# Where the modulation sums run: out of the attention's column projections, unevenly over the three branches, with a prioritised final addition

## The chip, the cores and the metric

The kernel runs on one core of a Trainium2 chip. A core has a matrix engine (TensorE, PE in the profile, with its weight loads as PEld), VectorE (DVE), ScalarE (ACT), GpSimd (POOL), and SyncE (SP), which here only issues transfers. Each engine has a queue of its own and works through it in order; they wait for one another by semaphores. The metric is the device time of one execution in microseconds (us); lower is better.

## What is computed

One layer of a conditioned decoder trunk in float32, 512 tokens of width 1024. From the conditioning vector `c` come six modulation vectors, and the layer uses them as shift, scale and gate of its two halves:

```python
mod = (c @ ada_w[l] + ada_b[l])[:, None, :]          # c: 1024, ada_w: 1024 x 6144
sh1, sc1, g1, sh2, sc2, g2 = jnp.split(mod, 6, axis=-1)
h = rmsnorm(x, norm_mix[l]) * (1 + sc1) + sh1
z = h @ w_in[l]
...
o_attn = dsa_attention(z_attn, positions, rel_bias)   # per query the 128 best-scored keys
o_rwkv = rwkv7_mix(z_rwkv, ...)
o_conv = c_b * causal_dwconv(c_c * c_x, sc_conv_w[l])
gates = jax.nn.sigmoid(z_gate).reshape(b, s, N_BRANCH, D_MODEL)
merged = sum(gates[:, :, i] * (o @ w_branch[l, i]) for i, o in enumerate((o_attn, o_rwkv, o_conv)))
x = x + g1 * (merged @ w_o[l])
h = rmsnorm(x, norm_ffn[l]) * (1 + sc2) + sh2
x = x + g2 * conv_glu_ffn(h, ffn_w_up[l], ffn_conv_w[l], ffn_w_down[l])
```

`sh1` and `sc1` are needed at the start. `g1`, `sh2`, `sc2` and `g2`, the last two thirds of `mod`, are needed only once the three branches are merged. The change is about when these late ones are computed.

## The kernel before

**Matrix products.** Each weight tile is loaded by SP (`wraw`, L147 in `load_raw`, four buffers), rounded by ACT to a high half `whi` (L163), and the rest, the low half `wlo`, is made by a subtraction (L169): on POOL up to the last branch, on DVE in it (`lo_engine`). Activations are split in the same way. Each product is then three matmuls (L181 to L183), 512 columns each. `whi` and `wlo` have three buffers. Results go to PSUM banks, three named `mm` and five named `sd`.

**Modulation sums** (`ada_parts`, L200 to L226). A generator with 64 steps: eight groups of 512 outputs (four columns of `modc`), each of eight steps. One step has SP load 256 KB of `ada_w` into `xraw` (three buffers) and DVE multiply it by one column of `c` and add it to `acc` (L219 for the first step of a group, L221 for the other seven; two buffers of `acc`). At step k = 4 of the following group, `finish` sums the group over the partitions by four one-column matmuls (L206, into an `mm` bank) and DVE adds the bias (L207), which frees the bank.

Who calls the generator sets where a step stands: `att_cols`, the projection of q, k and the index queries to DRAM (`z_att`), does one step for each of the four column blocks of slot 1 (the keys); `branch`, which makes the gates and the output product of one branch, does four steps for each of its eight gate blocks. What is left runs out in later calls, which then do nothing. The calls before come to 4 in `att_cols`, 32 in `branch(1)`, 28 in `branch(2)`, none in `branch(0)`.

**Order of the program.** Projections; scoring of the index keys; the selection (L842 to L844): for each of three query blocks, 16 rounds of `max` (eight largest of each row, `m8`) and `match_replace` (mark them) on the score tile `sc`; the attention (L855 to L898): four head pairs, each with loads of `qs`, `kh` and `kl` on POOL's queue, and per query block a load of the bias `bt` on SP's, an addition of the mask on POOL (L869), score matmuls (L817), the logits on DVE (L876), the exponential on ACT (L878), transposes on PE (L885), and the value product; then `branch(1)` (RWKV), `branch(2)` (convolution), `branch(0)` (attention), and the feed-forward half.

The written order is only a priority. A scheduler lays the instructions into the engines' queues, by program order as priority and by when operands are ready; `tc.high_priority(offset=...)` moves a piece ahead. So `branch(1)`, `branch(2)` and the steps called in them fill the queues beside the selection and the attention, which stand earlier in the program: in the order built, `branch(1)` runs during the selection and parts of `branch(2)` and its modulation steps lie before, in and behind the attention.

Of the kernel before, what the change touches and what calls it, by code (L numbers as in the profile page):

```python
# [16 lines left out]
ALU = mybir.AluOpType  # L17
# [42 lines left out]
def hybrid_block(ctx, tc, ins, out, consts, dbg=None, stop=99):  # L60
    nc = tc.nc
    PE, ACT, DVE, POOL, SP = nc.tensor, nc.scalar, nc.vector, nc.gpsimd, nc.sync
# [7 lines left out]
    def dram(name, offset, ap):  # L70
        t = ins[name]
        return bass.AP(tensor=t.tensor, offset=t.offset + offset, ap=ap)

    def mm_bank():
        return pp.tile([128, 512], F32, name="mm", tag="mm", bufs=3)

    def sd_bank():
        return pp.tile([128, 512], F32, name="sd", tag="sd", bufs=5)

    def T(name, shape, dt=F32, tag=None, bufs=1, pool=None):  # L80
        return (pool or sb).tile(shape, dt, name=name, tag=tag or name, bufs=bufs)
# [49 lines left out]
    def cv(name, i=0, n=1):  # L131
        tag, r = col[name]
        return colv[tag][:, r + i:r + i + n]
# [7 lines left out]
    def load_raw(shape, srcs, own=None):  # L141
        if own is None:
            raw = wp.pool.tile(shape, F32, name="wraw", tag="wraw", bufs=n_raw)
        else:
            raw = own[0].tile(shape, F32, name="xraw", tag="xraw", bufs=own[1])
        for dst, ap in srcs:
            SP.dma_start(dst(raw), ap)  # L147
        return raw
# [26 lines left out]
    def mm_t(ps, w, act, k0=0, start=True, stop=True):  # L175

        hi, lo = w
        ahi, alo = act
        kt = hi.shape[1]
        for k in range(kt):  # L180
            PE.matmul(ps, hi[:, k, :], ahi[:, k0 + k, :], start=start and k == 0, stop=False)  # L181
            PE.matmul(ps, hi[:, k, :], alo[:, k0 + k, :], start=False, stop=False)  # L182
            PE.matmul(ps, lo[:, k, :], ahi[:, k0 + k, :], start=False, stop=stop and k == kt - 1)  # L183
# [12 lines left out]
    def wk():  # L196
        return T("wk", [128, 512], tag="wk", bufs=4)


    def ada_parts():  # L200


        def finish(acc, o):
            pm = mm_bank()
            for i in range(4):
                PE.matmul(pm[:, i:i + 1], acc[:, i * 128:(i + 1) * 128], one, start=True, stop=True)  # L206
            DVE.tensor_tensor(modc[:, o:o + 4], pm[:, 0:4], cv("ada_b", o, 4), op=ALU.add)  # L207
            if o == 36:
                DVE.scalar_tensor_tensor(modc[:, 32:40], modc[:, 32:40], 1.0, cv("norm_ffn", 0, 8), op0=ALU.add, op1=ALU.mult)

        done = None
        for o in range(16, 48, 4):
            acc = T("acc", [128, 512], pool=adp.pool, bufs=2)
            for k in range(8):
                raw = load_raw([128, 512], [((lambda r: r), dram("ada_w", k * 128 * 6 * D + o * 128, [[6 * D, 128], [1, 512]]))],
                               own=(adp.pool, 3))
                ck = ccol[:, k:k + 1]
                if k == 0:
                    DVE.tensor_scalar(acc, raw, ck, None, op0=ALU.mult)  # L219
                else:  # L220
                    DVE.scalar_tensor_tensor(acc, raw, ck, acc, op0=ALU.mult, op1=ALU.add)  # L221
                if done and k == 4:
                    finish(*done)
                yield
            done = acc, o
        yield  # L226
        finish(*done)

    ada = ada_parts()

    def rsqrt_of(v, n):
# [25 lines left out]
    modc = T("modc", [128, 48])  # L257
# [50 lines left out]
    pm = sd_bank()  # L308
# [97 lines left out]
    def z_col(c0, n=128):  # L406
        w = w_in(c0, n)
        ps = mm_bank()
        mm_t(ps[:n], w, hT)
        return ps  # L410
# [50 lines left out]
    for p in range(4):  # L461
        i = p % 2
# [11 lines left out]
        k, r, kn, km, P, iP = (E(n, [128, 512]) for n in ("k", "r", "kn", "km", "P", "iP"))  # L474
# [51 lines left out]
        for c0 in (0, 4):  # L526
            for hh in range(2):
                q = halves[hh][0]
                ps = sd_bank()
                for c in range(c0, c0 + 4):  # L530
                    o = (c - c0) * 128
# [21 lines left out]
        for c0 in (0, 4):  # L553
            ps = sd_bank()
            for c in range(c0, c0 + 4):
                o = (c - c0) * 128
# [27 lines left out]
    for rnd in range(2):  # L584
        for u0 in (0, 16):
            ps = sd_bank()
            for u in range(u0, u0 + 16):
                for hh in range(2):
                    b = hh * 64
                    o = slice((u - u0) * 32, (u - u0) * 32 + 32)  # L590
# [15 lines left out]
    for c in range(8):  # L606
# [19 lines left out]
        for p in range(4):  # L626
            for hh in range(2):
                o = (p * 2 + hh) * 64
# [14 lines left out]
        if c:  # L643
            for p in range(4):
                for hh in range(2):
                    q, z = halves[hh]
                    o = (p * 2 + hh) * 64
# [107 lines left out]
    def split_out(dst, ps, scale):  # L755
        n = ps.shape[0]
        hi = T("wk", [128, 512], F32R, tag="wk", bufs=4)
        lo = T("wk", [128, 512], F32R, tag="wk", bufs=4)
        ACT.activation(hi[:n], ps, AF.Copy, scale=scale)
        DVE.scalar_tensor_tensor(lo[:n], ps, scale, hi[:n], op0=ALU.mult, op1=ALU.subtract)  # L760
        ACT.dma_start(dst[:, 0, :], hi[:n].bitcast(F32))
        SP.dma_start(dst[:, 1, :], lo[:n].bitcast(F32))

    def att_cols(c0, slot, scale):
        for i in range(4):
            if slot == 1:
                next(ada, None)
            if slot < 2:
                next(bias, None)
            split_out(z_att[slot, i], z_col(c0 + i * 128), scale)  # L770

    def load_q(dst, z, t0, n):

        row = 2 * 512
        for hh in range(2):
            src = bass.AP(tensor=z.tensor, offset=z.offset + hh * 512 + t0, ap=[[row, 64], [64 * row + (1 - 2 * hh) * 512, 2], [1, n]])
            POOL.dma_start(dst[hh * 64:(hh + 1) * 64], src)

    att_cols(C_ATT + 3 * MIX, 2, HD ** -0.5)
    ps = z_col(C_ATT + 4 * MIX, 72)  # L780
    split_out(z_ki, ps[0:64], 1.0)
# [129 lines left out]
    def branch(i, o, first, last):  # L911
        for m2 in range(4):
            gate = []
            for m in range(2):
                ps = z_col(C_GATE + i * D + (m2 * 2 + m) * 128)
                sg = wk()
                if first:
                    ACT.activation(sg, ps, AF.Sigmoid)
                else:
                    ACT.activation(sg, ps, AF.Tanh, scale=0.5)  # L920
                for _ in range(4):
                    next(ada, None)
                gate.append(sg)
            for m in range(2):
                mm = m2 * 2 + m
                w = weights("w_branch", i * MIX * D, D, 0, 4, [(mm * 128, 128)])
                ps = mm_bank()
                mm_t(ps, w, o)
                dst = merged[:, mm, :]
                if first:  # L930
                    ACT.activation(dst, ps, AF.Copy, scale=2.0)  # L931
                    POOL.tensor_tensor(dst, dst, gate[m], op=ALU.mult)
                    continue
                DVE.scalar_tensor_tensor(gate[m], gate[m], 1.0, ps, op0=ALU.add, op1=ALU.mult)
                DVE.tensor_tensor(dst, dst, gate[m], op=ALU.add)
                if last:
                    ACT.activation(mg_hl[0][:, mm, :], dst, AF.Copy, scale=0.5)
                    DVE.scalar_tensor_tensor(mg_hl[1][:, mm, :], dst, 0.5, mg_hl[0][:, mm, :], op0=ALU.mult, op1=ALU.subtract)

    def split_o(src):  # L940
# [4 lines left out]
        return o  # L945

    branch(1, split_o(o_rw), True, False)
    branch(2, split_o(o_cv), False, False)
    lo_engine[0] = DVE
# [376 lines left out]
```

## Time and profile before

| what | us |
| --- | --- |
| median of three runs | 1160.54 |
| the three runs | 1160.04, 1160.54, 1165.31 |
| the profiled execution, its own time | 1152.93 |
| span of that execution (first to last instruction) | 1150.9 |
| mean granted TensorE clock of that execution | 0.968 |

The profile shows one execution, hence its own time, below the median. The stretches of that execution that matter here: the last selection runs on DVE from about 465 to 515 us; the attention on PE from 534 to 626; the last branch, `branch(0)`, from 640 to 707. A busy share is an average over stages; a wait counts where PE, which is busy nearly throughout, has one.

### The profile page before, as it was taken

Reading aid. Unit: us, or ns where it says so; the run is one execution under the profiler, and the core shown is the slowest. Engines: PE = TensorE matmul, PEld = TensorE weight load, DVE = VectorE, ACT = ScalarE, POOL = GpSimd, SP = SyncE. Lnnn points to the kernel's source line nnn. Section 1 sums busy time; section 2 is a strip of 40 time slices with the busy share of each in tenths; the row PEclk is TensorE's granted clock in tenths of the full one; section 3 lists DMA queues with packets and bytes.
Section 4 is the critical chain, followed back from the end, with each engine's and each line's share of the span. In section 5 each row is a group of like instructions: output and inputs, shape, how many; then the busy total and the mean of one; then the engine's idle time right before and its main releaser. Section 6 shows DMA issues by size and latency. Waiting matters only on the chain.

```text
span 1150.9 us, 17786 instructions
## 1 busy us (share of the span) xinstructions
PE 1066.1 (93%) x6822; PEld 877.9 (76%) x6822; DVE 715.9 (62%) x1331; ACT 467.8 (41%) x786; POOL 342.0 (30%) x259
## 2 busy tenths in 40 slices
PE   4889999999899999977889999988999999999996
PEld 3667788777666877855678888878988898888885
DVE  5847766432699769993534435579767666652316
ACT  4255544332334344233444334356434443542213
POOL 4211111222363235654555000125344545100001
PEclk9789999999999999988899999998999999999999
DMA  9764467922548952689875334531333233462201
GB/s 328 199 147 97 106 130 161 217 73 75 133 125 248 284 166 67 183 225 243 210 157 168 104 91 139 154 110 38 92 111 97 65 95 101 157 219 92 92 1 73
DMA packets 194689, 160.32 MB, mean 139 GB/s; under 512 B 18563, under 2 KB 167453, under 8 KB 194605
## 3 DMA queue, kind: packets, MB, share of 16 engines
q1 hardware_dynamic: 162589, 122.55, 37.1%
q0 software_dynamic: 8960, 22.11, 9.9%
q10 hardware_dynamic: 23056, 14.53, 4.1%
q8 instruction: 53, 0.87, 0.3%
q14 instruction: 31, 0.25, 0.1%
HBM read 129.53 MB, written 18.63 MB: 129 GB/s over the span
## 4 chain that ended last, share of the span: by engine, by line
PE 62%; DVE 15%; DMA 9%; issue 8%; POOL 3%; ACT 3%; SPq 0%; POOLq 0%; DVEq 0%; ACTq 0%
PE mm L181 8%; PE mm L182 8%; PE mm L183 8%; DMA wraw<-in_ffn_w_up 2%; DMA xraw<-in_ada_w 2%; PE sd L181 2%; PE sd L182 2%; PE sd L183 2%; PE sd L1250 2%; PE sd L1252 2%; PE sd L1251 2%; PE sd L734 1%; DVE wlo L1017 1%; DMA bt<-bias_d 1%; PE sd L1047 1%
## 5 line engine op out<-in xcount | busy, mean ns | idle before, releaser
L182 PE MATMUL mm<-h_lo,whi 128*128 128x512 f32 (+2 forms) x496 | 198.3, 400 | 1.6 <-DVE h_lo L1076 1.5
L181 PE MATMUL mm<-h_hi,whi 128*128 128x512 f32 (+2 forms) x496 | 198.9, 402 | 0.3 <-ACT merged L931 0.3
L183 PE MATMUL mm<-h_hi,wlo 128*128 128x512 f32 (+2 forms) x496 | 198.6, 401 | 0.0
L163 ACT ACTIVATE whi<-wraw 128x1024 fp32r<-128x1024 f32 (+1 forms) x86 | 80.3, 935 | 204.3 <-PE mm L182 116.9
L169 POOL TENSOR_TENSOR wlo<-wraw,whi 128x1024 fp32r<-128x1024 f32 (+2 forms) x49 | 115.9, 2367 | 150.3 <-ACT whi L163 138.6
L182 PEld LDWEIGHTS mm<-h_lo,whi 128*128 128x128 f32 (+1 forms) x496 | 93.9, 189 | 21.1 <-DVE h_lo L1076 2.0
L183 PEld LDWEIGHTS mm<-h_hi,wlo 128*128 128x128 f32 (+1 forms) x496 | 94.0, 189 | 19.4 <-issue 0.2
L181 PEld LDWEIGHTS mm<-h_hi,whi 128*128 128x128 f32 (+1 forms) x496 | 93.7, 189 | 19.1 <-ACT merged L931 0.8
L1017 DVE TENSOR_TENSOR wlo<-wraw,whi 128x1024 fp32r<-128x1024 f32 x46 | 64.9, 1411 | 61.1 <-ACT whi L1016 60.4
L1016 ACT ACTIVATE whi<-wraw 128x1024 fp32r<-128x1024 f32 x46 | 48.6, 1057 | 78.6 <-DMA wraw<-in_ffn_w_up 28.1
L221 DVE SCALAR_TENSOR_TENSOR acc<-xraw,ccol,acc 128x512 f32<-128x512 f32 x56 | 62.9, 1122 | 26.0 <-DMA xraw<-in_ada_w 25.7
L1034 POOL TENSOR_TENSOR fS<-wraw 128x512 f32<-128x512 f32 x13 | 20.3, 1565 | 180.1 <-DVE wk L991 108.2
L1047 PE MATMUL sd<-mg_hi,shi 128*128 128x256 f32 x156 | 45.2, 289 | 8.9 <-DVE p L1190 8.9
L167 POOL DMA_DIRECT2D wlo<-wraw x21 | 18.2, 867 | 116.9 <-ACT wlo L166 111.7
L728 DVE TENSOR_SCALAR mk<-posq,thr 128x512 f16<-128x512 f32 (+3 forms) x128 | 47.1, 441 | 2.0 <-PE sd L734 2.0
L1017 DVE TENSOR_TENSOR slo<-wraw,shi 128x1024 fp32r<-128x1024 f32 x28 | 34.7, 1239 | 21.4 <-ACT shi L1016 21.4
L1293 POOL TENSOR_TENSOR f<-f 128x512 f32<-128x512 f32 x4 | 5.7, 1417 | 135.0 <-ACT wk L993 135.0
L181 PE MATMUL mm<-o,whi 128*128 128x512 f32 x96 | 39.9, 416 | 6.2 <-DVE modc L207 6.2
L181 PE MATMUL sd<-h_hi,whi 128*128 128x512 f32 x112 | 45.4, 405 | 0.0
L182 PE MATMUL sd<-h_lo,whi 128*128 128x512 f32 x112 | 45.3, 404 | 0.0
L183 PE MATMUL sd<-h_hi,wlo 128*128 128x512 f32 x112 | 45.0, 402 | 0.0
L1049 PE MATMUL sd<-mg_hi,slo 128*128 128x256 f32 x156 | 44.6, 286 | 0.0
(525 smaller groups left out, 2813.2 us busy)
## 6 DMA issues: line engine op xcount, KB each, us to landing
wraw<-in_w_in SPq DMA_DIRECT2D x61, 512.0 KB, 4.7
xraw<-in_ada_w SPq DMA_DIRECT2D x96, 256.0 KB, 4.2
wraw<-in_ffn_w_up SPq DMA_DIRECT2D x44, 512.0 KB, 4.2
wraw<-in_ffn_w_down SPq DMA_DIRECT2D x22, 512.0 KB, 3.5
wlo<-wraw POOLq DMA_DIRECT2D x21, 512.0 KB, 5.3
wraw<-in_w_branch SPq DMA_DIRECT2D x24, 256.0 KB, 3.1
bias_d<-stage ACTq DMA_DIRECT2D x10, 512.0 KB, 7.3
wraw<-in_w_o SPq DMA_DIRECT2D x8, 512.0 KB, 3.8
```

The lines of the kernel that those rows point to most:

```text
L163: ACT.activation(hi, raw, AF.Copy)
L169: lo_engine[0].tensor_tensor(lo, raw, hi, op=ALU.subtract)
L181: PE.matmul(ps, hi[:, k, :], ahi[:, k0 + k, :], start=start and k == 0, stop=False)
L182: PE.matmul(ps, hi[:, k, :], alo[:, k0 + k, :], start=False, stop=False)
L183: PE.matmul(ps, lo[:, k, :], ahi[:, k0 + k, :], start=False, stop=stop and k == kt - 1)
L221: DVE.scalar_tensor_tensor(acc, raw, ck, acc, op0=ALU.mult, op1=ALU.add)
L728: DVE.tensor_scalar(m_[:, :n], posq[:, b * 128:], thr[:, b, gg:gg + 1], None, op0=ALU.is_ge)
L1016: ACT.activation(hi, src, AF.Copy)
L1017: DVE.tensor_tensor(lo, src, hi, op=ALU.subtract)
L1047: PE.matmul(ps, w[0][:, k], b[0][:, k], start=first and k == 0, stop=False, skip_group_check=True)
L1049: PE.matmul(ps, w[1][:, k], b[0][:, k], start=False, stop=k == 3, skip_group_check=True)
L1250: PE.matmul(ps, hi, w[0][:, c], start=first, stop=False)
```

## The change

It does four things. `finish` is called at the end of the following group's eight steps in place of after the fifth. Its bias addition is issued with high priority. `att_cols` no longer calls the generator. And each gate block of a branch calls it three times in `branch(0)`, once in `branch(1)` and five times in `branch(2)`, in place of four times: 8 steps in `branch(1)`, 40 in `branch(2)`, the last 16 and the end in `branch(0)`.

```diff
-            DVE.tensor_tensor(modc[:, o:o + 4], pm[:, 0:4], cv("ada_b", o, 4), op=ALU.add)
+            with tc.high_priority(offset=4000):
+                DVE.tensor_tensor(modc[:, o:o + 4], pm[:, 0:4], cv("ada_b", o, 4), op=ALU.add)
...
-                if done and k == 4:
+                if done and k == 7:
                     finish(*done)
...
     def att_cols(c0, slot, scale):
         for i in range(4):
-            if slot == 1:
-                next(ada, None)
             if slot < 2:
                 next(bias, None)
...
-                for _ in range(4):
+                for _ in range((3, 1, 5)[i]):
                     next(ada, None)
```

Line numbers shift by one from L208 on and back by one from L766 on. In the orders below, rows are one instruction each, in the sequence of the engine's queue.

VectorE, the last of the three selections, before; `sc` is the score tile, `m_4558` the eight maxima:

```order
L207 TENSOR_TENSOR modc<-mm,colvA 128x4
L842 MAX m_4558<-sc 128x8
L219 TENSOR_SCALAR acc<-xraw,ccol 128x512
L843 MATCH_REPLACE sc<-m_4558,sc 128x512
L221 SCALAR_TENSOR_TENSOR acc<-xraw,ccol,acc 128x512
```

VectorE at the same place, the end of the selection and the beginning of the attention, after; `o<-o_cv,o` makes the low half of the convolution branch's input, the L875 rows are the first logits:

```order
L841 MAX m_4545<-sc 128x8
L842 MATCH_REPLACE sc<-m_4545,sc 128x512
L843 TENSOR_SCALAR sc<-sc 128x512
L943 TENSOR_TENSOR o<-o_cv,o 128x512 x4
L875 ISA lg,rs<-sd,bt 128x128
L875 ISA rs 128x1
```

Three groups of modulation steps and three final additions have left the selection, and the eight steps that stood between it and the first logits have gone too. Of the 64 steps 16 now stand before the scoring as they did, 16 in the attention (at the turns to its second and fourth head pair, as before), 8 at its end, and 24 behind it.

GpSimd, the first loads of the attention, before; L932 applies the gates of the first branch, `wlo` are low halves of weights:

```order
L169 TENSOR_TENSOR wlo<-wraw,whi 128x512
L932 TENSOR_TENSOR merged<-merged,wk 128x512
L777 DMA qs<-z_att 64x2x512 x2
L169 TENSOR_TENSOR wlo<-wraw,whi 128x512
L863 DMA kh<-z_att 64x2x512 x2
L863 DMA kl<-z_att 64x2x512 x2
L169 TENSOR_TENSOR wlo<-wraw,whi 128x1024
```

GpSimd at the same place, after:

```order
L931 TENSOR_TENSOR merged<-merged,wk 128x512
L169 TENSOR_TENSOR wlo<-wraw,whi 128x512
L776 DMA qs<-z_att 64x2x512 x2
L862 DMA kh<-z_att 64x2x512 x2
L169 TENSOR_TENSOR wlo<-wraw,whi 128x1024
L862 DMA kl<-z_att 64x2x512
L169 TENSOR_TENSOR wlo<-wraw,whi 128x1024
L862 DMA kl<-z_att 64x2x512
```

The loads of `kh` moved ahead of a subtraction; each of the two loads of `kl` now stands behind one more.

VectorE, the start of the last branch, before; `wk<-wk,mm` and `merged` apply a gate to a finished product:

```order
L944 TENSOR_TENSOR o<-o_at,o 128x512 x4
L169 TENSOR_TENSOR wlo<-wraw,whi 128x512
L169 TENSOR_TENSOR wlo<-wraw,whi 128x1024
L934 SCALAR_TENSOR_TENSOR wk<-wk,mm 128x512
L935 TENSOR_TENSOR merged<-merged,wk 128x512
```

VectorE at the same place, after:

```order
L943 TENSOR_TENSOR o<-o_at,o 128x512 x4
L222 SCALAR_TENSOR_TENSOR acc<-xraw,ccol,acc 128x512 x2
L169 TENSOR_TENSOR wlo<-wraw,whi 128x512
L222 SCALAR_TENSOR_TENSOR acc<-xraw,ccol,acc 128x512 x5
L169 TENSOR_TENSOR wlo<-wraw,whi 128x1024
L933 SCALAR_TENSOR_TENSOR wk<-wk,mm 128x512
L934 TENSOR_TENSOR merged<-merged,wk 128x512
```

Modulation additions now stand in front of the subtractions that make the weights of the last branch; two more such rows, of six and of five, follow later in it.

## Rows read from the trace of the kernel before

**Rows 1.** The page's first part: busy time, share of span, instructions of each engine.

```profile
PE 1066.1 (93%) x6822; PEld 877.9 (76%) x6822; DVE 715.9 (62%) x1331; ACT 467.8 (41%) x786; POOL 342.0 (30%) x259
```

**Rows 2.** The chain that ended last: start us, us, what ran there.

```profile
476.57 0.74 DVE sc L843 x2
477.31 2.16 DVE acc L221
```

**Rows 3.** Stretches: us, busy of PE, PEld, DVE, ACT, POOL, clock, DMA share, GB/s.

```profile
533.86:625.60 91.74, 83.30 (x473) 67.55 (x473) 42.51 (x120) 42.90 (x110) 49.65 (x39) 0.93 0.77 185
640.00:707.00 67.00, 67.00 (x291) 54.21 (x290) 30.84 (x42) 23.31 (x34) 0.00 (x0) 1.00 0.36 102
484.40:533.86 49.46, 35.43 (x138) 27.66 (x137) 39.84 (x66) 12.17 (x20) 24.26 (x19) 0.86 0.92 229
```

**Rows 4.** Timeline of VectorE, last selection: start us, us, instruction, idle before and releaser.

```profile
464.68 0.69 DVE L842 MAX8 m<-sc 128x8 f32<-128x512 f32 x1 [0.18 <-POOL sc L838]
...
508.75 0.68 DVE L842 MAX8 m<-sc 128x8 f32<-128x512 f32 x1
...
510.26 0.69 DVE L842 MAX8 m<-sc 128x8 f32<-128x512 f32 x1
...
514.25 0.41 DVE L844 TENSOR_SCALAR sc<-sc 128x512 f32<-128x512 f32 x1
```

**Rows 5.** L221 alone, that selection: us, VectorE busy, clock, DMA share, GB/s.

```profile
463.90:510.30 46.40, 26.15 (x21) 0.93 0.66 193
```

**Rows 6.** Timeline of TensorE, before and around the attention.

```profile
484.42 0.48 PE L181 MATMUL mm<-h_hi,whi 128*128 128x512 f32 x1
...
489.88 0.40 PE L183 MATMUL mm<-h_hi,wlo 128*128 128x512 f32 x1
496.45 0.80 PE L181 MATMUL mm<-o,whi 128*128 128x512 f32 x1 [6.18 <-DVE modc L207]
497.04 0.63 PE L182 MATMUL mm<-o,whi 128*128 128x512 f32 x1
497.47 0.63 PE L183 MATMUL mm<-o,wlo 128*128 128x512 f32 x1
...
522.59 0.80 PE L817 MATMUL sd<-kh,qs 128*128 128x256 f32 x2 [5.56 <-DMA kh<-z_att]
...
533.86 0.33 PE L885 MATMUL sd<-ident,lg 128*128 128x128 f32 x1 [2.29 <-ACT lg L878]
...
549.85 0.66 PE L885 MATMUL sd<-ident,lg 128*128 128x128 f32 x4 [1.22 <-ACT lg L878]
...
631.06 0.95 PE L206 MATMUL mm<-one,acc 128*128 128x1 f32 x8
631.86 0.48 PE L181 MATMUL mm<-h_hi,whi 128*128 128x512 f32 x1
```

**Rows 7.** GpSimd and ScalarE before the attention; landing times of `kh`, then `kl`.

```profile
484.33 1.30 POOL L169 TENSOR_TENSOR wlo<-wraw,whi 128x512 fp32r<-128x512 f32 x1 [0.57 <-ACT whi L163]
...
501.27 1.06 ACT L163 ACTIVATE whi<-wraw 128x1024 fp32r<-128x1024 f32 x1 [9.61 <-PE mm L182]
...
502.41 2.46 POOL L169 TENSOR_TENSOR wlo<-wraw,whi 128x1024 fp32r<-128x1024 f32 x1 [8.81 <-DMA xraw<-in_ada_w]
...
DMA to landing us min/median/max: 3.6/5.9/9.5
...
DMA to landing us min/median/max: 3.5/6.3/11.2
```

**Rows 8.** L221 by shape; landing of `xraw`; VectorE's L169; SyncE's queue, 440 to 640.

```profile
L221 DVE SCALAR_TENSOR_TENSOR acc<-xraw,ccol,acc x56: 724/752/2909, 329.6 to 610.7; 128x512 f32<-128x512 f32 x56
...
DMA to landing us min/median/max: 2.6/4.2/8.8
...
672.89 1.23 DVE L169 TENSOR_TENSOR wlo<-wraw,whi 128x1024 fp32r<-128x1024 f32 x1 [5.34 <-ACT whi L163]
...
SPq L147 <- DVE acc L221: 34.6, 31, 3.0
```

## The prediction

> **What bounds the kernel now.** I read the page first, then the chain that ended last, then the table of stretches, and last the timelines of VectorE (DVE), TensorE (PE) and GpSimd (POOL) between 464 and 640 us. The page has PE busy for 93% of the span [rows 1], so the end can only come nearer where PE waits or runs slowly. It does so around the selection: in the chain, selection steps (L843) alternate with additions of the modulation (L221), both on DVE [rows 2]. The stretches show the rest [rows 3]. From 484.4 to 533.9 PE is busy 35.4 us of 49.5 at a granted clock of 0.86, in the attention (533.9 to 625.6) 83.3 of 91.7 at 0.93, in the last branch (640 to 707) 67.0 of 67.0 at full clock. A gain made before 640 therefore reaches the end, since what follows waits on PE alone.
>
> On DVE the last selection (512 columns, 16 rounds) begins at 464.68 and ends at 514.66. A round with nothing between its two steps takes 1.51 us (508.75 to 510.26) [rows 4], so 16 take 24.2. Of the rest, 26.2 us are 21 additions L221 [rows 5].
>
> On PE [rows 6]: a block of 24 matmuls starts at 484.42; the first ends at 484.90, the last (489.88) at 490.28, so the 23 between take 5.38 us, 0.23 each (I reckon with 0.233). Then 6.18 us of idleness until DVE's final addition L207 frees a PSUM bank, 5.56 until kh lands, 2.29 before the first transpose L885 at 533.86. [...]
>
> **The change, part by part.**
>
> *Selection.* Three modulation groups (24 steps) leave DVE's queue between the rounds. The selection then ends near 464.7 + 24.2 + 0.4 = 489.3, which is 25.4 us earlier. That is not the gain: at 489 PE is still in the first branch, and what is late next is PE's own queue and the loads of kh and kl. L207 stood behind additions and selection steps; three of its matmul groups (L206) also leave this stretch, at 0.80 us of PE each (631.06 to 631.86 [rows 6]). So the block of 484.42 starts 2.4 us earlier, at 482.0, and the 6.18 us wait has no cause left.
>
> *Start of the attention on PE.* From that block to the first L885 the built order before holds 124 projection matmuls, that after 75 (all such numbers of matmuls below are counted in the two orders), since the scheduler now puts the attention in before the second branch. 75 x 0.233 + 0.5 for the four score matmuls = 18.0, hence 500.0 without a wait. kh is queued on POOL behind the subtraction that ran at 484.33 for 1.30 us, and behind qs. With all 2.4 us earlier qs starts at 483.2, kh by about 484.6, and with the median landing of 5.9 us it is there at 490.5, before PE asks at 491.8. kl stands behind two more subtractions, and each of these waits until PE frees a weight buffer: the second frees at 482.0 + 36 x 0.233 = 490.4, then a cast of 1.06 and, behind the first subtraction and one kl, a subtraction of 2.46 give 494.2. With the median landing of 6.3 us kl is there at 500.5 [rows 7]. PE asks at 482.0 + 62 x 0.233 + 0.3 = 496.7: a wait of 3.8 us (0 with the shortest landing of 3.5 and an early POOL, 8.7 with the longest, 11.2). I take the median, since that load has others beside it, as before. One fall of the clock is added, 1.7. The first L885 comes at 500.0 + 3.8 + 1.7 = 505.5 in place of 533.9: **-28.4**.
>
> *Attention.* Its matmuls are the same; the fillers between them are 143 in place of 139, with three L206 groups in place of two: 4 x 0.233 + 0.8 = **+1.7**. Before, two modulation groups fall into the attention behind its start (at the turn to the second and to the fourth head pair); after, two stand at the same two turns and a third begins at the end. So I leave its 8.4 us of PE idleness, but for the gap of 1.22 at 549.85 [rows 6], which follows a bias load queued behind modulation loads; in the first head pair these are gone: **-1.2** (ends: -8.4 and +8.4).
>
> *What PE still owes.* Fewer fillers went before the attention, so more come behind it: 118 matmuls in place of 73 up to the last branch, 45 x 0.233 = **+10.5**, and five L206 groups in place of two, **+2.4**.
>
> *Last branch.* Its 288 matmuls stay. New are 24 additions on DVE, which there also makes the low halves of the weights (L169). DVE is busy 30.8 of 67 us [rows 3]; 24 x 0.75 = 18 fit. They fit less well in order: six, five and five stand in a row in front of an L169, and with three buffers the fourth load of a row is issued only when the first is used, so a row costs about one landing (4.2 us [rows 8]) and 4 to 5 us of additions, some 8 to 9. Before, L169 runs as early as its buffer allows, since it waits 5.34 us for a cast that itself waits for the buffer [rows 8], so PE has two weight tiles ahead (12 + 24 matmuls, 8.4 us). Following the order step by step I find one place where cover and delay are equal. I take **+1.0** (ends 0 and 3 x 5).
>
> *Priority and place of the final addition.* It is one operation on four columns, and now comes as soon as its matmuls are done: nothing more, since its worst case is the wait already taken away. The modulation is still complete before the rows that use it (L971) are built behind the last branch; if it were not, PE would stand there for one landing and eight matmuls, 5 us.
>
> [...] Where they go the stretches show room [rows 3]: 24 loads of 256 KB (6.3 MB) in 67 us are 94 GB/s on top of 102, below the 229 GB/s seen at 484 to 534. [...]
>
> *Sum.* -28.4 + 1.7 - 1.2 + 10.5 + 2.4 + 1.0 = **-14.0 us**. The profiled execution took 1152.93 us (span 1150.9), so it would take 1138.9. The median of the three runs before is 1160.54, 7.6 above the profiled one; the forecast is a median, so **1146.5 us**, a range of its own from 1140 to 1152.
>
> **Rivals.**
>
> *The attention runs clear.* With the selection done 11 us before its first use and no modulation loads in the first head pair, neither kl nor the bias loads are waited for: 3.8 + 1.7 + 7.2 + 1.0 go as well, -27.7, 1132.8 us. For it: the loads of the start landed slowly under modulation loads (DMA share 0.92 [rows 3]). Against: two groups stay in the attention.
>
> *The last branch gives it back.* Each of the three rows of additions on DVE makes L169 late by 2.5 us, and PE pays this and the lower clock (1.7): 12.6 in place of 1.0, total -2.4, 1158.1 us. For it: no slack at one place. Against: POOL is idle from 640 to 707 [rows 3], and additions range from 0.72 to 2.91 us [rows 8], the mean in the selection being 26.15 / 21 = 1.25 with POOL at work. [...]
>
> *Slower.* SP's queue is in order, and a modulation load waits there until DVE frees a buffer (34.6 us in 31 waits between 440 and 640 [rows 8]), with bias and weight loads behind it. After the change 40 such loads stand between attention and weight loads. At 1.1 us each that is 44 us; if half of it outlasts the prefetch, +22 and one more fall of the clock make -14 + 24 = +10, 1170 us. It decides once a row of loads lasts longer than the 8.4 us of weights ahead.
>
> *It does not do what it says.* The scheduler could leave additions in the selection; the built order shows none, so this has almost no chance.
>
> **How the numbers follow.** Forecast 0.60; attention clear 0.15; last branch gives it back 0.15; slower 0.08; other 0.02. The range reaches from a half-clear attention to the give-back: **1135 to 1158**. A measurement of this kernel can tell about 0.5%, 5.8 us. Faster (below 1154.7): the forecast, the clear attention and a fourth of the give-back, 0.79; within: 0.13; slower: 0.08.
>
> **What would show it.** In the new trace the last selection should end within 4 us of 489; the first L885 should start at 500 to 508; the PE wait on L207 at 490 should be gone and one on kl stand in its place; the attention should last 88 to 96 us; from its end to the last branch some 29 us; and the last branch 67 to 69 us with PE fully busy. Wrong I am if kl or kh lands over 9 us after its issue, if the attention grows because bias loads sit behind modulation loads, or if L169 waits for additions.

## The result, and the profile after

The changed kernel takes 1143.37 us (median of four runs, 1141.1 to 1144.21) against 1160.29 for the kernel before in the same group; the ratio is 0.9889 with a 95% interval from 0.9845 to 0.9933. A second group of runs on another occasion gave 1138.64 against 1155.72, ratio 0.9858 (0.9823 to 0.9892). So the change makes the kernel 12.9 and 16.4 us faster by these ratios, 16.9 and 17.1 by the medians; forecast was 14.0. The kernel before varies from 1150 to 1165 us between its runs, so single profiles are compared here only where they differ by more than 2 us, or where several agree.

The engines do the same work as in [rows 1]; only the span is shorter. The page's first part, after:

```profile
PE 1063.5 (93%) x6822; PEld 876.1 (77%) x6822; DVE 716.2 (63%) x1331; ACT 467.5 (41%) x786; POOL 342.0 (30%) x259
```

The chain that ended last, after, in the stretch where [rows 2] showed selection steps and modulation additions in turn (start us, us, what):

```profile
488.14 0.24 PE mm L183
488.63 0.58 POOL kh L862
489.21 6.64 DMA kh<-z_att
495.90 0.50 PE sd L816 x2
...
497.48 5.41 DMA kl<-z_att
503.02 0.47 PE sd L817 x2
```

No step of the last selection is in it any more: it runs along PE's projection matmuls, then through the loads of `kh` and `kl`. The timeline of VectorE, after, answers [rows 4]:

```profile
468.59 0.69 DVE L841 MAX8 m<-sc 128x8 f32<-128x512 f32 x1 [1.43 <-POOL sc L837]
...
492.16 0.68 DVE L842 MATCH_REPLACE8 sc<-m,sc 128x512 f32<-128x512 f32 x1
492.87 1.98 DVE L843 TENSOR_SCALAR sc<-sc 128x512 f32<-128x512 f32 x1
499.52 4.32 DVE L943 TENSOR_TENSOR o<-o_cv,o 128x512 fp32r<-128x512 f32 x4 [4.67 <-ACT o L942]
```

The sixteen rounds take 24.3 us (468.59 to 492.87), as forecast, and afterwards VectorE sits idle for 4.67 us: the selection is not what the attention waits for. The timeline of TensorE, after, answers [rows 6]:

```profile
495.90 0.50 PE L816 MATMUL sd<-kh,qs 128*128 128x256 f32 x2 [0.83 <-DMA kh<-z_att]
503.02 0.47 PE L817 MATMUL sd<-kl,qs 128*128 128x256 f32 x2 [1.77 <-DMA kl<-z_att]
506.37 0.27 PE L884 MATMUL sd<-ident,lg 128*128 128x128 f32 x1
...
647.44 0.50 PE L183 MATMUL mm<-h_hi,wlo 128*128 128x512 f32 x1 [0.85 <-DVE wlo L169]
```

The 6.18 us wait for the final addition and the 5.56 us for `kh` are gone; 0.83 and 1.77 us stand in their place. In stretches (us, busy time of PE, PEld, DVE, ACT and POOL, clock, DMA share, GB/s), first of the kernel after, from the first transpose to the attention's end and from there to the last low half of the merged product, then the second of these stretches before:

```profile
506.40:601.00 94.60, 85.58 (x488) 69.32 (x486) 51.15 (x122) 42.95 (x110) 54.41 (x45) 0.93 0.70 177
601.00:703.70 102.70, 101.85 (x470) 83.33 (x469) 64.16 (x90) 32.98 (x47) 8.45 (x6) 1.00 0.63 188
```

```profile
625.80:714.30 88.50, 88.50 (x401) 72.29 (x400) 39.95 (x55) 29.95 (x43) 4.54 (x6) 1.00 0.40 119
```

The attention starts 27.5 us earlier (506.37 against 533.86 in [rows 6]), lasts 94.6 us (91.9 before), and 102.7 us follow in place of 88.5. What lies behind takes 438.0 (1141.7 - 703.7) against 436.6 (1150.9 - 714.3). The sum: -27.5 + 2.7 + 14.2 + 1.4 = -9.2, the difference of the two profiled spans. The second profile of the same changed kernel, with a span of 1134.4 us, reads:

```profile
506.80:598.10 91.30, 81.46 (x488) 65.77 (x487) 51.09 (x121) 42.41 (x108) 53.24 (x45) 0.98 0.70 178
598.10:700.30 102.20, 101.82 (x470) 83.40 (x469) 64.56 (x91) 32.98 (x47) 8.45 (x5) 1.00 0.63 189
```

The start and the stretch behind the attention repeat within 0.5 us; the attention is 3.3 us shorter, at a granted clock of 0.98 in place of 0.93, and the rest 3.9 us shorter. Between these two profiles it is the attention and what follows the merge that vary.

### The profile page after: what moved, and what is told of

The parts are those of the page before. It is cut to its first block, busy times and chain, and to the rows that moved or that the text cites. A ratio compares the mean times of both kernels' runs of the same rounds, so it can differ in the third digit from the quotient of the medians.

```text
span 1141.7 us, 17794 instructions
## 1 busy us (share of the span) xinstructions
PE 1063.5 (93%) x6822; PEld 876.1 (77%) x6822; DVE 716.2 (63%) x1331; ACT 467.5 (41%) x786; POOL 342.0 (30%) x259
## 4 chain that ended last, share of the span: by engine, by line
PE 59%; DVE 16%; DMA 10%; issue 9%; POOL 3%; ACT 3%; SPq 0%; POOLq 0%; DVEq 0%; ACTq 0%
PE mm L183 8%; PE mm L181 8%; PE mm L182 8%; DMA wraw<-in_ffn_w_up 3%; DMA xraw<-in_ada_w 2%; PE sd L1249 2%; PE sd L1251 2%; PE sd L1250 2%; PE sd L181 2%; PE sd L182 2%; PE sd L183 2%; DVE wlo L1016 2%; PE sd L735 1%; PE mm L1250 1%; PE mm L1251 1%
## 5 line engine op out<-in xcount | busy, mean ns | idle before, releaser
L169 POOL TENSOR_TENSOR wlo<-wraw,whi 128x1024 fp32r<-128x1024 f32 (+2 forms) x49 | 115.8, 2366 | 145.4 <-ACT whi L163 144.2
L222 DVE SCALAR_TENSOR_TENSOR acc<-xraw,ccol,acc 128x512 f32<-128x512 f32 x56 | 57.9, 1035 | 32.8 <-DMA xraw<-in_ada_w 32.2
L729 DVE TENSOR_SCALAR mk<-posq,thr 128x512 f16<-128x512 f32 (+3 forms) x128 | 44.8, 425 | 4.4 <-PE sd L735 4.4
L1047 PE MATMUL sd<-mg_lo,shi 128*128 128x256 f32 x156 | 44.6, 286 | 0.0
```

Of the source, the lines that this page charges most:

```text
L169: lo_engine[0].tensor_tensor(lo, raw, hi, op=ALU.subtract)
L729: DVE.tensor_scalar(m_[:, :n], posq[:, b * 128:], thr[:, b, gg:gg + 1], None, op0=ALU.is_ge)
L1047: PE.matmul(ps, w[0][:, k], b[1][:, k], start=False, stop=False, skip_group_check=True)
```

## The experiments

### One part of the change at a time

The final addition alone, in the kernel before:

```diff
-            DVE.tensor_tensor(modc[:, o:o + 4], pm[:, 0:4], cv("ada_b", o, 4), op=ALU.add)
+            with tc.high_priority(offset=4000):
+                DVE.tensor_tensor(modc[:, o:o + 4], pm[:, 0:4], cv("ada_b", o, 4), op=ALU.add)
...
-                if done and k == 4:
+                if done and k == 7:
```

> The kernel before with the two edits of the final addition alone (priority, and behind the eighth step in place of the fifth). Theory: the time does not move (0 +- 3 us against the kernel before). In the built order only the first of the three final additions of the selection changes its place, and the additions of the modulation still stand between the selection's steps, so the selection still ends near 515, the first transpose L885 still starts near 534, and PE still waits for a final addition near 490. Rival, that the gain of the change is this wait: 6.2 us of idleness and 1.7 us of the lower clock go, 6 to 8 us faster.

Measured: ratio 0.9998 (0.9958 to 1.0037). The timeline of TensorE in this kernel still has the wait:

```profile
494.86 0.79 PE L181 MATMUL mm<-o,whi 128*128 128x512 f32 x1 [6.17 <-DVE modc L208]
```

The forecast holds. The edit that names the final addition does nothing by itself: its wait comes from the additions and selection steps that stand ahead of it on VectorE (one of these additions takes 2.82 us, from 489.74), and these stay.

The split over the branches alone, in the kernel before:

```diff
-                for _ in range(4):
+                for _ in range((3, 1, 5)[i]):
                     next(ada, None)
```

> The kernel before with the uneven split over the branches alone (3, 1 and 5 steps per gate block); the attention's columns still call four steps, the final addition is as before. Theory: nearly all of the change's gain, 10 to 14 us faster than before. In the built order no modulation step is left in the selection, 199 projection matmuls stand between the scoring and the first transpose of the attention (250 before), so that transpose starts near 506; the attention holds three groups of modulation steps in place of two and lasts 93 to 98 us; the last branch holds 8 steps. Rival, that the four steps called in the attention's columns are what delays the selection: under 5 us faster.

Measured: ratio 0.9871 (0.9828 to 0.9914), 14.9 us by the ratio, as much as the whole change within the intervals and as forecast. The attention runs from 506.7 to 600.6; the second line is the stretch behind it:

```profile
506.70:600.60 93.90, 83.78 (x489) 66.97 (x488) 56.29 (x130) 42.93 (x108) 54.25 (x44) 0.96 0.79 199
600.60:701.00 100.40, 100.40 (x461) 82.31 (x460) 59.29 (x81) 33.20 (x47) 8.50 (x6) 1.00 0.57 171
```

The attention's columns alone, in the kernel before:

```diff
     def att_cols(c0, slot, scale):
         for i in range(4):
-            if slot == 1:
-                next(ada, None)
```

> The kernel before without the four steps that the attention's columns call, nothing else. 19 of the 24 steps stay in the selection, and 240 projection matmuls stand ahead of the first transpose in place of 250. Theory: a small gain, 3 us (between 6 faster and 1 slower); the selection ends some 6 us earlier (five additions of 1.25), the first transpose starts 4 to 8 us earlier, and a large part of this is given back by matmuls that come behind the attention. Rival, that these four steps are what the change gains by: 10 us or more.

Measured: ratio 1.002 (0.9993 to 1.0047), no gain. The start was right: the first transpose comes at 530.0 in place of 533.9. But the attention then takes 99.0 us:

```profile
530.00:629.00 99.00, 85.38 (x487) 70.07 (x486) 58.16 (x127) 42.85 (x108) 54.07 (x42) 0.93 0.75 185
```

Here 21 modulation steps run in the attention (16 in the same stretch before), the first three of them between its second and its third logit, and it lasts 7.1 us longer. So the small gain that was forecast is lost in the attention; that the added steps are the reason is not shown by this run alone.

So one edit of the four carries the change, and the other three add nothing to it that can be measured.

### Modulation steps in the attention, and behind it

Another split of the changed kernel, run twice:

```diff
-                for _ in range((3, 1, 5)[i]):
+                for _ in range((6, 0, 3)[i]):
```

> The changed kernel with another split: 6 steps per gate block in the attention's branch (the last), 0 in the first and 3 in the convolution's. In the built order the start of the attention is that of the changed kernel, no modulation step is left in the attention, 11 stand between it and the last branch and 37 in it (15 in the changed kernel). Theory: the attention's 9.0 us of PE idleness are its own chain (logits, exponential, transpose, product), so it stays within 2 us of the changed kernel's 94.6; in the last branch the rows of additions in front of L169 cost PE 1 to 4 us more; total 8 to 13 us faster than the kernel before, at or just above the changed kernel. Rival, that the attention runs clear without modulation loads: 7 us less there, 18 to 20 us faster than before. Rival, that the last branch gives the gain back: each row of additions costs 2.5 us and the lower clock, 0 to 4 us faster than before.

> 6, 0 and 3 steps per gate block a second time, for a direct comparison. Theory: without modulation steps the attention lasts 80 to 84 us (94.6 in the changed kernel), and the stretch behind it 108 to 114 us (102.7), so it is 2 to 7 us faster than the changed kernel in the same call. Rival, that the stretch behind takes all of it back, as with 7, 0 and 3 and with the late convolution steps, where PE waited 10.0 and 5.4 us for the last sum: 0 to 5 us slower than the changed kernel.

> The changed kernel itself, a second time, beside the next one on the same chip. Both theories: 0.7 to 1.6% faster than the kernel before; the first transpose at 505 to 508, the attention 93 to 97 us, the stretch behind it up to the last low half 101 to 105 us.

Measured: 0.9863 (0.981 to 0.9916), and in the second group 0.986 (0.9829 to 0.989) beside 0.9858 (0.9823 to 0.9892) for the changed kernel. The two splits cannot be told apart. The stretches of the first and then of the second profile:

```profile
504.60:585.60 81.00, 76.35 (x460) 61.26 (x459) 27.08 (x100) 42.48 (x110) 51.06 (x41) 1.00 0.67 150
585.60:696.90 111.30, 108.30 (x503) 88.81 (x502) 77.88 (x112) 33.26 (x48) 11.70 (x9) 0.98 0.69 213
```

```profile
508.60:593.70 85.10, 79.10 (x460) 63.87 (x459) 27.08 (x100) 42.14 (x109) 50.78 (x41) 0.96 0.65 138
593.70:707.20 113.50, 110.62 (x502) 90.77 (x501) 77.62 (x111) 33.38 (x48) 11.64 (x9) 0.95 0.67 209
```

The rival "attention runs clear" was right about the attention: without modulation steps it takes 81.0 and 85.1 us in place of 94.6 and 91.3. My theory that its idleness is its own chain falls, and with 15.8 us by the ratio the first run came out above the 8 to 13 us forecast. But the stretch behind takes 9 to 11 us back, 111.3 and 113.5 us in place of 102.7 and 102.2. The larger part is TensorE's own work: the stretch now holds 503 matmuls in place of 470, and PE is busy in it for 108.3 us in place of 101.9. The timeline of TensorE in the first profile shows a second cause near the end of the last branch:

```profile
677.27 0.65 PE L970 MATMUL sd<-ident,modc 128*128 128x128 f32 x4 [1.36 <-DVE modc L208]
679.57 0.61 PE L206 MATMUL mm<-one,acc 128*128 128x1 f32 x4 [1.65 <-DVE acc L222]
```

PE waits for the last sums themselves, 3.0 us together. The forecast that this split beats the changed kernel by 2 to 7 us was wrong, and the rival that the stretch behind takes all of it back was right. Of the forecasts for the changed kernel's second run those for the start (506.8 us) and for the stretch behind the attention (102.2) came true; its attention, 91.3 us, was shorter than the 93 to 97 expected.

Two splits that call the last steps earlier, both of the changed kernel:

```diff
-                for _ in range((3, 1, 5)[i]):
+                for _ in range((7, 0, 3)[i]):
```

```diff
-                for _ in range((3, 1, 5)[i]):
+                for _ in range((3, 3, 3, 3, 2, 6, 8, 8)[2 * m2 + m] if i == 2 else (6, 0)[i]):
```

> The changed kernel with 7 steps per gate block in the last branch, 0 in the first, 3 in the convolution's. As with 6, 0 and 3, no step is left in the attention and 37 stand in the last branch, but the last of them stands some three weight tiles earlier. Theory: the attention lasts 80 to 82 us; the 3.0 us for which PE waited near the end of the last branch for the last sum (1.4 for the last final addition, 1.65 for the last addition) go, and with them part of the low clock: 1 to 5 us faster than with 6, 0 and 3, 1.5 to 2.0% faster than the kernel before. Rival, that denser rows of additions delay L169 instead: as long as with 6, 0 and 3, or up to 5 us longer.

> The changed kernel with 6 steps per gate block in the last branch, 0 in the first, and in the convolution's 3, 3, 3, 3, 2, 6, 8, 8 over its eight gate blocks. No step in the attention; 19 between it and the last branch, 29 in the last branch, the last of them some four weight tiles ahead of its end. Theory: the attention lasts 80 to 82 us, and the stretch from its end to the last low half of the merged product takes 104 to 107 us (111.3 with 6, 0 and 3; 102.7 in the changed kernel): 4 to 7 us faster than with 6, 0 and 3, 1.7 to 2.2% faster than the kernel before. Rival, that the stretch between attention and last branch becomes bound by its loads (its DMA share is 0.90 in the changed kernel already): PE waits there 3 us or more, and nothing is won over 6, 0 and 3.

Measured: 0.9941 (0.9917 to 0.9966) and 0.9949 (0.9922 to 0.9976), both slower than the changed kernel in its second group (0.9858, 0.9823 to 0.9892). Both forecasts, each a gain over 6-0-3, were wrong. Attentions of 83.3 and 82.4 us again, and stretches of 120.7 and 123.7 us behind them. TensorE's largest waits, 7-0-3 first and then the late convolution steps (there PE also waits 2.62 and 2.28 us for earlier sums, and the granted clock of the stretch is 0.93):

```profile
681.17 1.84 PE L206 MATMUL mm<-one,acc 128*128 128x1 f32 x8 [10.04 <-DVE acc L222]
```

```profile
677.68 1.86 PE L206 MATMUL mm<-one,acc 128*128 128x1 f32 x8 [5.43 <-DVE acc L222]
```

The last sum does come earlier, but not by as much as its matmuls were moved ahead. From the attention's end to its first matmul, 6-0-3 takes 94.0 us with 428 matmuls of PE in between, 7-0-3 takes 91.4 with 380, and the late convolution steps 88.5 with 356. The 48 matmuls between the first two are 11.2 us of PE at 0.233 us each (an estimate from the block in [rows 6]); the sum came 2.6 us earlier. The loads of the modulation tiles in 7-0-3 are spread like this (the line of `xraw`'s loads: count; time on the queue, min/median/max in ns; first and last start in us):

```profile
L147 SPq DMA_DIRECT2D xraw<-in_ada_w x45: 327/328/581, 596.6 to 677.4; - x45
```

That is (677.4 - 596.6) / 44 = 1.84 us for a step, and (675.8 - 592.4) / 44 = 1.90 in 6-0-3 (1.76 with the late convolution steps). The stream of steps keeps about the same rate, while the scheduler has put the summing matmuls L206 earlier into PE's queue. PE then stands, for 10.04 us in 7-0-3 and 5.43 with the late convolution steps, until the stream has caught up.

What sets the rate was tried by issuing these loads from GpSimd's queue in the last branch, on top of 7-0-3:

```diff
-            SP.dma_start(dst(raw), ap)
+            (POOL if own and lo_engine[0] is DVE else SP).dma_start(dst(raw), ap)
```

> 7, 0 and 3 steps per gate block, and the modulation loads that are called in the last branch are issued by GpSimd's queue in place of SyncE's. With 7, 0 and 3 PE waited 10.0 us for the last addition at 681, since the stream of modulation steps ran at 1.85 us for each. Theory S, that SyncE's queue in order holds the stream (weight loads that wait there for a buffer, 30 us for L169 between 590 and 700, stand in front of modulation loads): the step takes 1.3 to 1.6 us, the wait of 10.0 us shrinks below 3, and the kernel is 6 to 11 us faster than with SyncE's queue. Theory R, that three buffers and one landing of 4 to 5 us set the step (3 loads in 5.6 us): the step stays at 1.7 to 2.0 us, the wait at 8 to 12, and the time within 3 us of it.

Measured: 0.9984 (0.9956 to 1.0011), no faster than 7-0-3 from SyncE (0.9941, 0.9917 to 0.9966, in another group). The loads of the last branch on the new queue, and PE's wait:

```profile
L147 POOL DMA_DIRECT2D xraw<-in_ada_w x40: 537/537/571, 605.7 to 681.9; - x40
```

```profile
686.02 1.84 PE L206 MATMUL mm<-one,acc 128*128 128x1 f32 x8 [9.59 <-DVE acc L222]
```

The step takes (681.9 - 605.7) / 39 = 1.95 us and the wait stays, both as theory R has it. So SyncE's queue in order (theory S) is not what sets the rate. An issue took 0.33 us on SyncE's queue and 0.54 on GpSimd's (the medians of the two lines of loads), and the steps of 1.84 and 1.95 us lie close.

That the three buffers and the landing (theory R) set it is not shown. Within PE's long wait in 7-0-3 the ring can be seen on VectorE: three additions, a wait for a tile, three additions, a wait for a tile, and the last one.

```profile
671.44 2.32 DVE L222 SCALAR_TENSOR_TENSOR acc<-xraw,ccol,acc 128x512 f32<-128x512 f32 x3
676.62 2.33 DVE L222 SCALAR_TENSOR_TENSOR acc<-xraw,ccol,acc 128x512 f32<-128x512 f32 x3 [2.85 <-DMA xraw<-in_ada_w]
680.27 0.75 DVE L222 SCALAR_TENSOR_TENSOR acc<-xraw,ccol,acc 128x512 f32<-128x512 f32 x1 [1.32 <-DMA xraw<-in_ada_w]
```

Over the whole run of steps, though, the median landing of `xraw` is only 3.4 us. With an addition of 0.75 and an issue of 0.33 that is 4.5 us for three steps, where 5.5 were measured. A rival is VectorE itself, which has the low halves and the gates in the same queue:

```profile
596.60:681.20 84.60, 73.16 (x347) 60.03 (x345) 64.04 (x91) 22.05 (x32) 8.00 (x4) 0.95 0.76 230
```

It is busy for 64.0 of these 84.6 us; of the rest it waits 12.8 us for tiles and 6.9 us, in front of final additions L208, for summing matmuls. A fourth buffer, the direct test of R, was not run, so the share of each stays open.

### Additions or loads

The attention's price for modulation steps was taken apart in the changed kernel; first without additions, then without loads:

```diff
                 else:
+                    if o in (24, 28) and k < 7: yield; continue
                     DVE.scalar_tensor_tensor(acc, raw, ck, acc, op0=ALU.mult, op1=ALU.add)
```

```diff
-                raw = load_raw([128, 512], [((lambda r: r), dram("ada_w", ...))],
+                if o not in (24, 28) or k == 0:
+                    raw = load_raw([128, 512], [((lambda r: r), dram("ada_w", ...))],
```

> The changed kernel with 12 of the 16 modulation additions that stand in the attention left out (steps 1 to 6 of the groups at outputs 24 and 28; their sums, and what hangs on them, are not the reference's); their loads are kept. The question is why the attention lasts 94.6 us in the changed kernel and 81.0 without any modulation step in it. Theory A, that the additions on VectorE do it (1.33 us each there, ahead of the logits in the same queue): the attention lasts 82 to 87 us. Theory L, that the loads do it (they stand in SyncE's queue among the bias loads and share the DMA engines): it stays at 91 to 95 us.

> The changed kernel with 14 of the 16 modulation loads that stand in the attention left out (the groups at outputs 24 and 28 use their first tile eight times; their sums, and what hangs on them, are not the reference's); all additions are kept. Theory A (the additions): the attention stays at 90 to 95 us. Theory L (the loads): it lasts 82 to 87 us. If both this and the run without additions shorten it by a part, both work.

The stretches of the attention, without additions and then without loads:

```profile
514.00:603.60 89.60, 80.54 (x476) 65.02 (x475) 29.91 (x106) 41.85 (x109) 51.19 (x41) 0.96 0.75 173
```

```profile
506.30:598.90 92.60, 83.22 (x483) 67.50 (x482) 50.57 (x120) 42.00 (x108) 52.55 (x41) 0.94 0.59 133
```

(The first profile is some 7 us late from before the scoring on; only the stretch's length is compared.) 89.6 and 92.6 us against 94.6 and 91.3: without additions neither theory's range was met, without loads that of theory A (the additions). Taking additions away shortens the attention by 2 to 5 us, taking loads away by nothing that stands out from the two profiles of the changed kernel, and taking both away, with the three groups of summing matmuls (0.95 us of PE each, L206) and four fillers, by 6 to 14. The loads alone are thus not it. The run without additions also has 12 matmuls fewer in the stretch than the changed kernel (476 against 488), which is up to 2.8 us of PE at 0.233 us each (an estimate), so less than the 2 to 5 us may belong to the additions. Whether they would do it without the four that were left in this kernel stays open. Neither kernel is faster than the changed one as a whole: 0.9866 (0.9822 to 0.991) and 0.9875 (0.9842 to 0.9907).

### Low halves of the last branch on GpSimd

```diff
-    lo_engine[0] = DVE
     branch(0, split_o(o_at), False, True)
```

> The changed kernel with the low halves of the last branch's weights (L169) on GpSimd in place of VectorE; TensorE's order is the same. In the changed kernel the additions took 1.33 us on average in the attention, where GpSimd works, and 0.75 in the last branch, where it does not. Theory: this is GpSimd's work beside VectorE's; with L169 on GpSimd the additions of the last branch take 1.0 to 1.4 us, L169 takes 2.4 us in place of 1.2, PE waits 1 to 6 us for it, and the kernel is 0 to 6 us slower than the changed kernel. Rival, that the additions are long in the attention for other reasons (their loads): they stay at 0.75, VectorE is rid of 15 us, PE's wait of 0.85 us for L169 goes, 0 to 3 us faster than the changed kernel.

Measured: 0.9908 (0.9872 to 0.9945), 1144.63 us, 6.0 above the changed kernel in the same group; the two intervals overlap, so the lost time is likely but not shown. The additions of the last branch by shape (busy us, mean ns of one), in the changed kernel and then here:

```profile
L222 DVE SCALAR_TENSOR_TENSOR acc<-xraw,ccol,acc 128x512 f32<-128x512 f32 x19 | 14.3, 750 | 10.3 <-DMA xraw<-in_ada_w 10.1
```

```profile
L222 DVE SCALAR_TENSOR_TENSOR acc<-xraw,ccol,acc 128x512 f32<-128x512 f32 x19 | 21.3, 1123 | 9.7 <-DMA xraw<-in_ada_w 9.3
```

TensorE's order is the same in both, and so are the additions; only L169 has moved. PE now waits 4.01 us for a final addition behind such additions:

```profile
630.49 0.68 PE L181 MATMUL mm<-o,whi 128*128 128x512 f32 x1 [4.01 <-DVE modc L208]
```

The theory holds for the additions, in size too (1.12 us, forecast 1.0 to 1.4). PE's wait has the size that was forecast, but it is for a final addition and not for L169.

Other VectorE operations of the same stretch separate in the same way, here in the kernel with L169 on GpSimd:

```profile
L937 DVE SCALAR_TENSOR_TENSOR mg_lo<-merged,mg_hi 128x512 fp32r<-128x512 f32 x6 | 7.0, 1169 | 4.2 <-ACT mg_hi L936 4.2
L933 DVE SCALAR_TENSOR_TENSOR wk<-wk,mm 128x512 f32<-128x512 f32 x8 | 5.4, 680 | 5.0 <-PE mm L183 5.0
```

L937, which reads two tiles in SBUF, took 688 ns in the changed kernel and takes 1169 here. L933 reads one of its two tiles from a PSUM bank (`mm`) and stays: 682 and 680 ns.

## Why the prediction was right

**What bounds.** Right. The selection left the chain, and what came late next was PE's own queue, then `kh` and `kl`, as named.

**Start of the attention, -28.4: measured -27.5.** The size is right by luck, since errors in it cancel. The working put the first L885 at 505.5, and it came at 506.4. Waits were 2.6 us (0.83 and 1.77) where 3.8 was taken, and the fall of the clock (1.7, my estimate from the trace before, where the matmuls from 497.04 to 500.46 start 0.43 us apart in place of 0.233, at a granted clock of 0.50) did not come in this profile (granted 1.00 from 492.9 to 506.4), though the second has a clock of 0.88 between the end of the selection's last round (492.1) and the first transpose, with matmuls 0.43 us apart from 503.45 to 506.44. Against that stand some 3.8 us that the sum doesn't have. PE's queue and VectorE's were both late by then: the selection began at 468.59, not at 464.68, and hence ended at 494.85, 5.5 us after the 489.3 of the forecast, outside the 4 us allowed. Most of the loss lies in the value projection at 390 to 418 us, which I had not looked at. From its first to its last matmul with `wlo`, in the kernel before, with the split alone, and in the changed kernel:

```profile
389.72:414.71 24.99, 22.89 (x191) 22.48 (x190) 11.23 (x11) 6.32 (x9) 7.86 (x3) 1.00 0.87 271
393.01:418.01 25.00, 22.88 (x191) 22.47 (x190) 11.86 (x10) 6.15 (x8) 7.54 (x3) 1.00 0.86 270
390.58:418.19 27.61, 24.66 (x192) 24.06 (x190) 9.47 (x11) 6.64 (x9) 7.66 (x3) 0.94 0.81 262
```

In the changed kernel PE waits longest in it for a weight's low half, 2.18 us against 1.52 in the kernel before, and then runs at a lower clock (0.94 over the stretch, 1.00 before):

```profile
406.99 0.39 PE L193 MATMUL mm<-wlo,h_hi 128*128 128x256 f32 x1 [2.18 <-POOL wlo L169]
```

The three profiles with the four calls in the attention's columns take 24.9 to 25.0 us for this projection, the eleven without them 25.4 to 28.7. The kernel with the split alone has lost the steps in the selection and keeps the 25.0 us, so this loss goes with the third edit, the calls taken out of `att_cols` (25.8 us with that edit alone), and not with the split that brings the gain. (The split kernel's selection begins late too, at 468.41, but it was 3.3 us late already at 334 us.) Why the calls matter there stays open.

**Attention, +0.5: measured +2.7 and -0.6.** The size came out near by the accident that before and after hold two groups of steps each. Its reasoning was wrong. I left the 8.4 us of idleness as the attention's own, and kernels without steps in the attention show that modulation makes 6 to 14 us of its length, idleness, summing matmuls and lower clock together. The rival "attention runs clear" named the right mechanism; it did not come because two groups stay.

**What PE still owes and the last branch, +10.5 + 2.4 + 1.0 = +13.9: measured +14.2 and +13.7.** Right in sum. The last branch was found with one tight place, 1.0 us; PE waits once for L169 there, 0.85 us. The parts came otherwise: from the attention's end to the last branch 28.3 us (601.0 to 629.28; some 29 forecast, 18.3 before), and the last branch 70.8 us (to 700.04) in place of 67 to 69, since the three added groups of summing matmuls stand in it and not ahead of it. The additions took 0.75 us each (750 ns, the mean of 19 in the last branch), as 24 x 0.75 had them.

**The rivals that lost.** "The last branch gives it back" and "slower by SyncE's queue" did not happen with 15 steps in the last branch. With 29 and 37 steps there, part of the gain is given back, but by another way than named: not through L169, but through matmuls moved behind the attention and through summing matmuls that wait for the stream of steps. SyncE's queue was not what held it.

**Priority and place of the final addition, 0.** Right, 0.9998.

The range 1135 to 1158 held both medians, 1143.37 and 1138.64. Of the 14.0 us forecast 12.9 and 16.4 came by the ratios, 16.9 and 17.1 by the medians.

## What to carry to other kernels

Work that fills gaps has a price where it is put and another where it was: count what the critical engine still owes before the gain of an earlier start is booked (here 27.5 us earlier, 14 owed back). A stream of small steps had a rate here (1.76 to 1.95 us for a step); where its consumers stood ahead of that rate in PE's queue, PE waited (10.04 us in 7-0-3), and calling the steps earlier made it worse. And when a change has four edits, try each alone: here one carried all.

## What the runs showed of the hardware

Some VectorE instructions took longer here where GpSimd computed, the additions L222 on two SBUF tiles among them. In the changed kernel's attention, where GpSimd is busy 54 of 95 us, their mean is 1332 ns:

```profile
L222 DVE SCALAR_TENSOR_TENSOR acc<-xraw,ccol,acc 128x512 f32<-128x512 f32 x16 | 21.3, 1332 | 5.4 <-DMA xraw<-in_ada_w 5.2
```

against 750 in the last branch without GpSimd and 1123 there with it. One of them, with GpSimd's timeline beside it:

```profile
522.20 4.77 DVE L222 SCALAR_TENSOR_TENSOR acc<-xraw,ccol,acc 128x512 f32<-128x512 f32 x1
```

```profile
522.80 2.37 POOL L169 TENSOR_TENSOR wlo<-wraw,whi 128x1024 fp32r<-128x1024 f32 x1
525.13 1.28 POOL L868 TENSOR_TENSOR bt<-bt,sc 128x512 f32<-128x512 f32 x1
```

The addition ends at 526.97, 0.56 us after the second of GpSimd's two operations. The rows have it begin 0.60 us before the first of them; why it lasts past both the runs do not show. The last step of the selection, an operation on one tile, shows it too: L843 took 1.98 us beside a subtraction on GpSimd (2.40 us from 492.17), in place of 0.41 in [rows 4]; the selection's `max` and `match_replace` kept their 0.69 and 0.68 us, with GpSimd busy 19.7 of 27.3 us from 468.6 to 495.9, and L933, which reads one of its tiles from PSUM, its 0.68. The means of 750 and 1123 ns come from the same additions and the same order on PE with L169 alone moved to GpSimd, so GpSimd's work lengthens them here; by what mechanism no run here isolates.
